# Two-layer hybrid trunk on one core: MLP down product as seven half-size products after the up products, hidden blocks and weight sums through DRAM and GpSimd; GLA level products of two heads together

## The chip, the cores and the metric

One core of one Trainium2 chip runs the whole program. The metric is device time in microseconds: the median of repeated executions. Lower is better. Engines work side by side, each through its own instructions in order: TensorE (matmuls; in the profile PE, its weight loads PEld), VectorE (DVE), ScalarE (ACT), GpSimd (POOL), and SyncE (SP), which issues the DMAs here.

## What is computed

Two layers over 1024 rows of width 1024. Each layer adds a token mixer (layer 0: forgetting attention and Mamba-2; layer 1: stick-breaking attention and gated linear attention, GLA) and then an MLP with 4096 hidden units; a norm ends it. The parts that the change touches:

```python
def squared_relu_mlp(h, w_up, w_down):
    u = jax.nn.relu(h @ w_up)
    return (u * u) @ w_down

def gla_chunked(q, k, v, log_a):
    ...
    attn = jnp.einsum('bcthk,bcshk,bctshk->bctsh', qc, kc, decay)
    o_intra = jnp.einsum('bctsh,bcshv->bcthv', attn, vc)
    ...
    return (o_intra + o_inter).reshape(b, L, H, V)

        h = h + mix.astype(h.dtype)
        u = rms_norm(h, norm_mlp[i])
        h = h + squared_relu_mlp(u, w_mlp_up[i], w_mlp_down[i]).astype(h.dtype)
```

## The kernel before

All of it stays in fp32 precision by splitting: an operand becomes a rounded part (a cast on ScalarE, line 78, `wh`) and a rest (a subtract on VectorE, line 79, `wl`), and each product takes three matmuls: high x high, high x low, low x high. A full matmul is 128 x 128 weights against 128 x 512 columns.

`mlp` (line 381) runs over 16 groups g of 256 hidden units. For a group, the up product is made from seven half-size products, P1 to P7, in the manner of Strassen and Winograd: P1 and P2 in `first(g)`, then P6, P5, P7, P4, P3 in `rest(g)`, each 12 matmuls in `prod` (line 395). The sums around them (s1, s2, s3, s4 of weight blocks; u2, u3, c11, c22 of results) are VectorE's, in `op` (line 407). `put` squares the rectified block (lines 400, 401) and splits it. The hidden blocks c11, u3, u2, c22 are the four quarters of the group's hidden values: 256 units by two halves of 512 rows.

After that `down(g)` multiplies them with the group's two rows of w_down blocks: 16 outputs (two halves of the columns, eight tiles of 128 rows), each 2 x 3 matmuls (lines 494 to 496), and VectorE adds each output into the resident `h` (line 498). `weights(g)` loads four blocks of w_down and splits them. In the order on TensorE, `first(g + 1)` stands ahead of `down(g)`, so the 96 down matmuls of a group run between P2 of the next group and its P6. After the last group `done(tb)` norms finished rows.

The order on each engine is the program's, rearranged by a list scheduler ahead of time; each engine runs its list strictly in order. Buffers come from pools with fixed numbers: `f` (5 blocks of 128 x 512), `q4` (4 pairs), `raw` (5), `wh` and `wl` (6 each). PSUM has eight banks under the names mm (three), av, sc (two), tr (two). A write into a buffer waits until all readers of its last content are done, a DMA that writes it out among them.

The GLA part (lines 876 to 909) works for two pairs of heads in chunks of 512 rows. For each of seven levels VectorE makes a difference M of cumulated gates (line 881), ScalarE takes two exponentials (884, 885), VectorE multiplies with keys and queries (886, 888), and TensorE multiplies M with itself, four 128-column pieces for the head in rows 0 to 63 and then four for the head in rows 64 to 127 (line 895); VectorE copies the result under a mask (line 900). Line 906 does an eighth product from keys and queries. Projection matmuls of the same layer (line 172) stand between these in TensorE's order.

Of the kernel before, what the change touches and what calls it, by code (L numbers as in the profile page):

```python
# [8 lines left out]
F32 = mybir.dt.float32  # L9
F32R = mybir.dt.float32r  # L10
# [23 lines left out]
class Net:  # L34
# [346 lines left out]
    def mlp(self, pool, h, wu, wd, E, scratch, done, late):  # L381
# [7 lines left out]
        T2, T3, T4 = ([E[:, i, j] for i in range(2)] for j in range(3))  # L389

# [8 lines left out]
        def put(c, hT, hf, m):  # L399
            nc.scalar.activation(c, c, AF.Relu)  # L400
            nc.scalar.activation(c, c, AF.Square)
            if hf not in hT:
                hT[hf] = [self.t(pool, [P, 2, HF], "q4", F32R, bufs=4) for _ in range(2)]
            self.split(hT[hf][0][:, m], hT[hf][1][:, m], c)

        def op(out, a, b, f):
            nc.vector.tensor_tensor(out=out, in0=a, in1=b, op=f)  # L407

# [14 lines left out]
        def first(g):  # L423
# [6 lines left out]
            p1 = F()  # L430
            nc.scalar.copy(p1, prod(get(), A11, B11))
            c11 = F()
# [3 lines left out]
        def rest(g, src, a11, a12, p1, c11, more):  # L436
            a21, a22, s1, s2, S2 = more or second(src, a11)
            hT = {}
# [7 lines left out]
            put(c11, hT, 0, 0)  # L446
# [13 lines left out]
            put(c22, hT, 1, 1)  # L460
# [6 lines left out]
            put(u3, hT, 0, 1)  # L467
            op(u2, u2, P3, ALU.add)
            put(u2, hT, 1, 0)
            return hT  # L470

        def weights(g):
            ws = {}
            for nh in range(2):
                for m in range(2):
                    r = self.raw([(0, HF, wd[g * G + m * P:g * G + (m + 1) * P,
                                             nh * HF:(nh + 1) * HF].unsqueeze(1))], 1, HF)
                    ws[nh, m] = self.wsplit(r, HF)
            return ws

        def down(g, hT, ws):
            last = g == NG - 1
            if last:
                S = scratch()
            order = [(nh, tb) for nh in range(2) for tb in range(NTB)]
            if last:
                order = [(nh, tb) for tb in range(NTB) for nh in range(2)]
            for nh, tb in order:
                ps = self.t(self.ps, [P, HF], "mm", bufs=NB["mm"])
                hf, o = tb // 4, (tb % 4) * P  # L490
                for m in range(2):
                    a, b = (x[:, m, o:o + P] for x in hT[hf])
                    wh, wl = ws[nh, m]
                    nc.tensor.matmul(ps, a, wh, start=m == 0, stop=False)  # L494
                    nc.tensor.matmul(ps, a, wl, start=False, stop=False)  # L495
# [575 lines left out]
```

## Time and profile before

| what | value |
|---|---|
| median of three runs | 2552.37 us (2550.16 to 2552.89) |
| profiled execution | 2552.78 us, its span 2550.9 us |
| TensorE matmuls | 2477.8 us busy, 97% of the span |
| VectorE | 1723.1 us, 68% |
| ScalarE | 1117.9 us, 44% |
| GpSimd | 179.3 us, 7% |
| DMA | 142.93 MB, mean 56 GB/s |
| mean granted TensorE clock | 0.993 |

The span is the time from the first to the last instruction of the profiled execution; 1.9 us lie around it. Busy shares are averages over stages with different limits. Matmuls overlap in the records: one takes 0.39 us from start to modelled end, but the next may start 0.23 us after it, so starts are what to count. The granted clock 1.00 is 2.4 GHz, 0.50 is 1.2 GHz.

### The profile page before, as it was taken

To read this page: it belongs to the slowest core of one execution; us is meant where nothing else is said; L and a number is where in the kernel's file an instruction comes from. 1 tells how busy PE (TensorE), PEld (TensorE's weight loads), DVE (VectorE), ACT (ScalarE), POOL (GpSimd) and SP (SyncE) were. 2 spreads that over 40 slices of the span, in tenths; PEclk is the share of its full clock that TensorE was granted. 3 is DMA by queue.
4 is the path that set the end of the run, shared out by engine and by line. 5 is a ranking of instruction groups with operands and counts; after the bars stand their busy time and mean duration, and the time that the engine had idled before them with its cause. 6 is when DMAs were issued, how large, how long until landed. Compare 5 with 4: busy or idle time off the path is not lost.

```text
span 2550.9 us, 33781 instructions
## 1 busy us (share of the span) xinstructions
PE 2477.8 (97%) x12734; PEld 2024.0 (79%) x12734; DVE 1723.1 (68%) x3056; ACT 1117.9 (44%) x2184; POOL 179.3 (7%) x282
## 2 busy tenths in 40 slices
PE   8999989999999999999998889999999999999998
PEld 7777776988888888888976678777988888888887
DVE  5787857577666666666669993676486666666666
ACT  4577646354232333333457665454252333323233
POOL 1111013000000000000113330000000000000000
PEclk9999998999999999999999999999999999999999
DMA  4212222202111111112211011102211111111112
GB/s 138 62 56 58 99 69 56 83 9 71 49 51 51 49 54 50 50 50 63 103 34 28 26 36 38 42 17 67 92 46 54 48 52 50 50 50 50 50 50 87
DMA packets 159922, 142.93 MB, mean 56 GB/s; under 512 B 14704, under 2 KB 130432, under 8 KB 159760
## 3 DMA queue, kind: packets, MB, share of 16 engines
q1 hardware_dynamic: 159760, 140.79, 18.6%
q8 instruction: 100, 1.64, 0.3%
q14 instruction: 62, 0.51, 0.1%
HBM read 128.11 MB, written 12.65 MB: 55 GB/s over the span
## 4 chain that ended last, share of the span: by engine, by line
PE 40%; issue 5%; DVE 3%; POOL 2%; ACT 1%; POOLq 0%; DVEq 0%; ACTq 0%
PE tr L395 5%; PE mm L172 5%; PE sc L395 5%; PE mm L495 4%; PE mm L494 4%; PE mm L496 4%; PE mm L156 3%; PE sc L172 2%; PE av L395 2%; PE sc L895 2%; POOL rr L790 1%; PE av L172 1%; DVE rr L792 1%; POOL pr L790 1%; POOL rs L123 0%
## 5 line engine op out<-in xcount | busy, mean ns | idle before, releaser
L498 DVE TENSOR_TENSOR h<-h,mm 128x512 f32<-128x512 f32 x512 | 350.1, 685 | 141.2 <-PE mm L496 135.2
L495 PE MATMUL mm<-wl,q 128*128 128x512 f32 x1024 | 403.9, 395 | 0.0
L494 PE MATMUL mm<-wh,q 128*128 128x512 f32 x1024 | 403.1, 394 | 0.0
L496 PE MATMUL mm<-wh,q 128*128 128x512 f32 x1024 | 402.0, 393 | 0.0
L78 ACT CAST wh<-raw 128x512 fp32r<-128x512 f32 (+1 forms) x340 | 210.1, 621 | 349.0 <-PE tr L395 124.2
L79 DVE TENSOR_TENSOR wl<-raw,wh 128x512 fp32r<-128x512 f32 (+1 forms) x340 | 232.7, 687 | 100.4 <-ACT wh L78 95.7
L156 PE MATMUL mm<-U,wh 128*128 128x512 f32 x832 | 279.1, 401 | 0.5 <-ACT xin L651 0.5
L78 ACT CAST wh<-f 128x512 fp32r<-128x512 f32 x128 | 76.4, 619 | 350.3 <-DVE h L498 325.6
L494 PEld LDWEIGHTS mm<-wh,q 128*128 128x128 f32 x1024 | 192.2, 188 | 45.7 <-ACT q L78 0.3
L496 PEld LDWEIGHTS mm<-wh,q 128*128 128x128 f32 x1024 | 192.4, 188 | 44.4
L495 PEld LDWEIGHTS mm<-wl,q 128*128 128x128 f32 x1024 | 192.3, 188 | 44.0
L172 PE MATMUL mm<-wh,U 128*128 128x256 f32 (+2 forms) x992 | 226.6, 312 | 0.2 <-ACT U L78 0.2
L156 PEld LDWEIGHTS mm<-U,wh 128*128 128x128 f32 x832 | 156.8, 190 | 32.2 <-issue 1.1
L172 PEld LDWEIGHTS mm<-wh,U 128*128 128x128 f32 x992 | 163.6, 189 | 14.4 <-issue 4.1
L156 PE MATMUL mm<-U,wl 128*128 128x512 f32 x416 | 167.8, 403 | 0.0
L123 POOL TENSOR_TENSOR rs<-ms,mhalf 128x1 f32<-128x1 f32 (+2 forms) x56 | 38.3, 685 | 1806.0 <-DVE ms L121 1806.0
L395 PE MATMUL tr<-U,wh 128*128 128x512 f32 x496 | 155.1, 394 | 0.0
L172 PE MATMUL mm<-wl,U 128*128 128x256 f32 (+2 forms) x496 | 153.8, 310 | 0.6 <-DVE wl L79 0.6
L395 PE MATMUL sc<-U,wh 128*128 128x512 f32 x480 | 150.4, 395 | 0.0
L78 ACT CAST q<-f 128x512 fp32r<-128x512 f32 x128 | 76.1, 616 | 144.3 <-PE mm L495 143.1
L407 DVE TENSOR_TENSOR f<-f,tr 128x512 f32<-128x512 f32 x124 | 82.4, 684 | 72.0 <-PE tr L395 72.0
L256 PE MATMUL tr<-ident,pr 128*128 128x128 f32 x576 | 100.3, 279 | 22.2 <-DVE pr L793 13.8
(312 smaller groups left out, 4912.3 us busy)
## 6 DMA issues: line engine op xcount, KB each, us to landing
raw<-in_w_mlp_up SPq DMA_DIRECT2D x128, 256.0 KB, 2.8
raw<-in_w_mlp_down SPq DMA_DIRECT2D x128, 256.0 KB, 2.7
raw<-in_w_in_ab SPq DMA_DIRECT2D x40, 256.0 KB, 3.0
raw<-in_w_in_cd SPq DMA_DIRECT2D x40, 256.0 KB, 2.9
xload<-in_x SPq DMA_DIRECT2D x8, 512.0 KB, 4.1
gb<-gd SPq DMA_DIRECT2D x8, 512.0 KB, 4.5
catT<-y SPq DMA_DIRECT2D x32, 128.0 KB, 2.2
h<-in_x SPq DMA_DIRECT2D x8, 512.0 KB, 6.2
```

The costliest lines, as they stand in the source:

```text
L78: self.nc.scalar.copy(hi, src)
L79: self.nc.vector.tensor_tensor(out=lo, in0=src, in1=hi.bitcast(F32), op=ALU.subtract)
L156: nc.tensor.matmul(ps, a, b[hf][:, kc], start=kc == 0 and i == 0, stop=kc == NKC - 1 and i == 2)
L172: nc.tensor.matmul(d, a, b, start=kc == 0 and i == 0, stop=kc == NKC - 1 and i == 2)
L256: nc.tensor.transpose(ps[:, k * P:(k + 1) * P], probs[k][:, j * P:(j + 1) * P], self.ident)
L395: nc.tensor.matmul(ps, a[:, kc], b[:, kc], start=kc == 0 and i == 0, stop=kc == 3 and i == 2)
L407: nc.vector.tensor_tensor(out=out, in0=a, in1=b, op=f)
L494: nc.tensor.matmul(ps, a, wh, start=m == 0, stop=False)
L495: nc.tensor.matmul(ps, a, wl, start=False, stop=False)
L496: nc.tensor.matmul(ps, b, wh, start=False, stop=m == 1)
L498: nc.vector.tensor_tensor(out=s, in0=s, in1=ps, op=ALU.add)
L790: nc.gpsimd.affine_select(d, d, [[-1, P]], ALU.is_gt, f, base=0, channel_multiplier=1)
```

## The change

**Up products.** `put` no longer splits. It writes c11, u3 and c22 to DRAM tiles `hid` (A11, A12, A22). After P3 GpSimd makes four sums of hidden blocks, t1 = u2 + c22, t2 = t1 - c11, t4 = u3 - t2, and c11 - u2; they are written to DRAM as S1, S2, S4, S3: seven blocks of 256 KB for each group. `down` and `weights` leave the loop. P1 and c11 now share a `q4` pair.

**Down product.** After all 16 groups a new `down` makes seven products over all 4096 hidden units, in the order S3, S1, S2, A22, A11, S4, A12. Six have 16 steps of 12 matmuls (one step for each group, summed in four PSUM banks); the last has two halves of 16 steps of 6. Each step loads its hidden block back from DRAM and a block of w_down (two for S3 and S1, 512 KB), in the products S3, S1, S2 and A22 GpSimd makes a difference of w_down blocks, and both operands are split (two casts, two subtracts). Up to three steps are split ahead. At the end of a product its banks are added into `h` or subtracted, 56 operations a layer in place of 256. `keep` holds 16 weight sums between products.

**GLA.** `intra` takes the two heads of a pair together, 128-column pieces in turn, into both sc banks. The level difference goes from VectorE to GpSimd, with three buffers gM in place of two. The output products of a chunk are regrouped. The value projection of layer 1 takes its row tiles in the order 4 to 7, 0 to 3.

```diff
@@ mlp
+        hid = {x: [self.t(self.dram, [P, HF], f"hid{x}{g}") for g in range(NG)]
+               for x in ("A11", "A12", "A22", "S1", "S2", "S3", "S4")}
...
-        def put(c, hT, hf, m):
+        def put(c, to, g):
             nc.scalar.activation(c, c, AF.Relu)
             nc.scalar.activation(c, c, AF.Square)
-            if hf not in hT:
-                hT[hf] = [self.t(pool, [P, 2, HF], "q4", F32R, bufs=4) for _ in range(2)]
-            self.split(hT[hf][0][:, m], hT[hf][1][:, m], c)
+            if to is not None:
+                nc.sync.dma_start(hid[to][g], c)
...
-            p1 = F()
+            two = self.t(pool, [P, 2, HF], "q4", bufs=4)
+            p1, c11 = two[:, 0], two[:, 1]
...
-            put(u2, hT, 1, 0)
-            return hT
...
+            put(u2, None, g)
+            two = self.t(pool, [P, 2, HF], "q4", bufs=4)
+            t1, t2, t4 = two[:, 0], two[:, 1], F()
+            pool_op(t1, u2, c22, ALU.add)
+            pool_op(t2, t1, c11, ALU.subtract)
+            pool_op(t4, u3, t2, ALU.subtract)
+            pool_op(u2, c11, u2, ALU.subtract)
+            for to, x in (("S1", t1), ("S2", t2), ("S4", t4), ("S3", u2)):
+                nc.sync.dma_start(hid[to][g], x)
...
-            hT = rest(g, *cur)
-            ws = weights(g)
+            rest(g, *cur)
             if g + 1 < NG:
                 cur = first(g + 1)
-            down(g, hT, ws)
+        self.down(pool, h, wd, hid, scratch, done)
...
+        def t3(k):
+            x = two(wd[k * G:(k + 1) * G, HF:].rearrange("(m p) c -> p m c", p=P))
+            return sub(x[:, 1], x[:, 1], x[:, 0])
...
+        plan = [("S3", t3, [(1, 0, ADD), (1, 1, ADD)]),
+                ("S1", t1, [(0, 1, ADD), (1, 1, ADD)]),
+                ("S2", t2, [(0, 1, ADD), (1, 0, ADD), (1, 1, ADD)]),
+                ("A22", t4, [(1, 0, SUB)]),
+                ("A11", lambda k: block(k, 0, 0), [(1, 0, ADD), (1, 1, ADD), (0, 0, ADD), (0, 1, ADD)]),
+                ("S4", lambda k: block(k, 1, 1), [(0, 1, ADD)]),
+                ("A12", lambda k: block(k, 1, 0), [(0, 0, ADD)])]
...
+        sets = [(mm, mm, mm, self.av), (self.sc, self.sc, self.tr, self.tr)]
+        steps = [(i, 0, 4, k) for i in range(6) for k in range(NG)]
+        steps += [(6, a, 2, k) for a in (0, 2) for k in range(NG)]
...
+            while len(ready) < 3 and s + len(ready) < len(steps):
+                ready.append(operands(*steps[s + len(ready)]))
...
+            for hf, nh, f in plan[i][2]:
+                for j in range(n):
+                    y = h[4 * hf + a + j][:, nh * HF:(nh + 1) * HF]
+                    nc.vector.tensor_tensor(out=y, in0=y, in1=ps[j], op=f)
@@ GLA
+            ps = [net.sc().rearrange("p (c l) -> p c l", l=P) for _ in range(2)]
+            for c in range(4):
+                for hh in range(2):
+                    rows, cs = slice(hh * 64, hh * 64 + 64), slice(c * P, (c + 1) * P)
+                    nc.tensor.matmul(ps[hh][:, c], kx[rows, cs], qx[rows, cs],
+                                     start=True, stop=True)
...
-                M = t(pool, [P, HF], "gM", bufs=2)
+                M = t(pool, [P, HF], "gM", bufs=3)
...
-                nc.vector.tensor_tensor(out=mv, in0=hv,
+                nc.gpsimd.tensor_tensor(out=mv, in0=hv,
...
@@ layer 1
-            for tb in range(NTB):
+            for tb in (4, 5, 6, 7, 0, 1, 2, 3):
```

Where the change moves instructions, in three places.

VectorE at the end of a group's up product, before: the first row is u2 += P3, then three splits of hidden blocks (`q4`) and one of weights; s1 is the row of two raw operands, s2 the next of line 407, s3 the last.

```order
1200 L407 TENSOR_TENSOR f_1919_8669<-f_1919_8669,tr_1964_8928 128x512
1201 L79 TENSOR_TENSOR q4_1961_8920<-f_1959_8915,q4_1960_8919 128x512
1202 L79 TENSOR_TENSOR q4_1950_8873<-f_1955_8895,q4_1949_8872 128x512
1203 L79 TENSOR_TENSOR wl_1982_8984<-raw_1978_8977,wh_1981_8983 128x512
1204 L79 TENSOR_TENSOR q4_1961_8920<-f_1919_8669,q4_1960_8919 128x512
1205 L407 TENSOR_TENSOR f_1985_9002<-f_1983_8987,sc_1986_9003 128x512
1206 L407 TENSOR_TENSOR f_2005_9149<-raw_2003_9145,raw_2004_9147 128x512
1207 L498 TENSOR_TENSOR h0_1002_3662<-h0_1002_3662,mm_1987_9017 128x512
1208 L407 TENSOR_TENSOR f_2006_9150<-f_2005_9149,raw_1977_8975 128x512
1209 L407 TENSOR_TENSOR f_2015_9194<-raw_1977_8975,raw_2003_9145 128x512
```

The same place after (another group): u2 += P3 in the first row, then s1, s2, s3 of the next group, then the split of S2 (from s2).

```order
913 L408 TENSOR_TENSOR q4_1634_6863<-q4_1634_6863,tr_1658_6987 128x512
914 L408 TENSOR_TENSOR f_1672_7062<-raw_1670_7058,raw_1671_7060 128x512
915 L408 TENSOR_TENSOR f_1673_7063<-f_1672_7062,raw_1661_7017 128x512
916 L408 TENSOR_TENSOR f_1680_7104<-raw_1661_7017,raw_1670_7058 128x512
917 L79 TENSOR_TENSOR wl_1675_7067<-f_1673_7063,wh_1674_7066 128x512
918 L408 TENSOR_TENSOR q4_1667_7029<-q4_1667_7029,sc_1669_7044 128x512
919 L79 TENSOR_TENSOR wl_1678_7084<-f_1672_7062,wh_1677_7083 128x512
```

The hidden splits and the adds into h are gone from here; row 916, s3, writes the buffer that held c22 of the group before, so it waits for GpSimd's t1 and for the write of A22, and row 917 stands behind it.

SP at the end of a layer's up products, after: writes of the last group's hidden blocks (`hid...15`), a first load of w_down, then reloads of hidden blocks (`f<-hidS3...`).

```order
307 L405 DMA hidA2215_1464_6274<-f_2051_8969 128x512
308 L405 DMA hidA1215_1448_6258<-f_2047_8949 128x512
309 L504 DMA q4_2061_9016<-in_w_mlp_down 128x2x512
310 L480 DMA hidS115_1480_6290<-q4_2055_8999 128x512
311 L480 DMA hidS215_1496_6306<-q4_2055_8999 128x512
312 L480 DMA hidS415_1528_6338<-f_2056_9000 128x512
313 L480 DMA hidS315_1512_6322<-q4_2030_8855 128x512
314 L540 DMA f_2058_9010<-hidS30_1497_6307 128x512
315 L540 DMA f_2064_9023<-hidS31_1498_6308 128x512
316 L504 DMA q4_2067_9029<-in_w_mlp_down 128x2x512
```

Before, SP had only loads of w_down blocks here (`raw<-in_w_mlp_down`, four for the last group); now the first reload, row 314, stands behind four writes that wait for GpSimd's sums.

VectorE at the end of product A11, after: the split of the second step of the product S4, the adds of A11 into h, and the splits of the third step. The 16 adds are rows 1324 to 1339; the middle ones are left out.

```order
1322 L79 TENSOR_TENSOR wl_2567_11051<-f_2565_11048,wh_2566_11050 128x512
1323 L79 TENSOR_TENSOR wl_2570_11057<-raw_2568_11054,wh_2569_11056 128x512
1324 L562 TENSOR_TENSOR h4_1006_3666<-h4_1006_3666,mm_2477_10696 128x512
1325 L562 TENSOR_TENSOR h5_1007_3667<-h5_1007_3667,mm_2478_10697 128x512
...
1338 L562 TENSOR_TENSOR h2_1004_3664<-h2_1004_3664,mm_2479_10698 128x512
1339 L562 TENSOR_TENSOR h3_1005_3665<-h3_1005_3665,av_2480_10699 128x512
1340 L79 TENSOR_TENSOR wl_2573_11091<-f_2571_11088,wh_2572_11090 128x512
1341 L79 TENSOR_TENSOR wl_2576_11097<-raw_2574_11094,wh_2575_11096 128x512
```

Before, such adds stood one at a time between other work, one for every six down matmuls; now they stand together between the splits of two steps.

TensorE in a GLA level: before, four matmuls of one head and four of the other; after, in 28 of the 32 such places, three, three, one, one (in four they alternate singly). First before, then after.

```order
6558 L172 MATMUL mm_3359_15903<-wl_3284_15553,U_3_76 128x512
6559 L895 MATMUL sc_3314_15636<-gM_3313_15630 128x128 x4
6560 L895 MATMUL sc_3315_15642<-gM_3313_15630 128x128 x4
6561 L172 MATMUL mm_3359_15903<-wh_3283_15552,U_3_76 128x512
6562 L172 MATMUL mm_3359_15903<-wh_3286_15558,U_3_76 128x512
```

```order
6387 L172 MATMUL mm_3772_16612<-wh_3693_16255,U_3_76 128x512
6388 L941 MATMUL sc_3727_16345<-gM_3726_16339 128x128 x3
6389 L941 MATMUL sc_3728_16346<-gM_3726_16339 128x128 x3
6390 L941 MATMUL sc_3727_16345<-gM_3726_16339 128x128
6391 L941 MATMUL sc_3728_16346<-gM_3726_16339 128x128
6392 L172 MATMUL mm_3772_16612<-wh_3696_16261,U_3_76 128x512
```

What moved is that the second head's matmuls now begin before the first head's are all issued.

## Rows read from the trace of the kernel before

**Rows 1.** Page, part 1: span; busy us, share, instructions of each engine.
```profile
span 2550.9 us, 33781 instructions
PE 2477.8 (97%) x12734; PEld 2024.0 (79%) x12734; DVE 1723.1 (68%) x3056; ACT 1117.9 (44%) x2184; POOL 179.3 (7%) x282
```

**Rows 2.** Page, part 5: line, engine, out<-in, count, busy, mean ns, idle before.
```profile
L498 DVE TENSOR_TENSOR h<-h,mm 128x512 f32<-128x512 f32 x512 | 350.1, 685 | 141.2 <-PE mm L496 135.2
...
L496 PE MATMUL mm<-wh,q 128*128 128x512 f32 x1024 | 402.0, 393 | 0.0
L78 ACT CAST wh<-raw 128x512 fp32r<-128x512 f32 (+1 forms) x340 | 210.1, 621 | 349.0 <-PE tr L395 124.2
L79 DVE TENSOR_TENSOR wl<-raw,wh 128x512 fp32r<-128x512 f32 (+1 forms) x340 | 232.7, 687 | 100.4 <-ACT wh L78 95.7
```

**Rows 3.** Chain of waits, one group's first two up products: start, us, what.
```profile
2006.54 5.55 PE tr L395 x24
```

**Rows 4.** Stretches: busy us of PE, PEld, DVE, ACT, POOL; PEclk; DMA share, GB/s.
```profile
2006.50:2048.20 41.70, 41.70 (x182) 33.87 (x181) 26.93 (x43) 13.92 (x24) 0.00 (x0) 1.00 0.17 51
...
1627.00:1673.00 46.00, 45.36 (x326) 36.24 (x324) 38.74 (x73) 16.99 (x34) 0.00 (x0) 1.00 0.04 12
...
369.50:375.60 6.10, 0.06 (x1) 0.00 (x0) 0.82 (x3) 2.36 (x10) 0.78 (x1) 0.83 0.77 176
375.60:387.20 11.60, 11.60 (x36) 8.64 (x37) 5.11 (x9) 8.46 (x23) 1.98 (x3) 0.50 0.60 93
433.80:435.80 2.00, 0.04 (x2) 0.03 (x1) 1.18 (x3) 1.98 (x6) 0.72 (x2) 0.79 0.38 56
435.80:445.30 9.50, 9.45 (x33) 8.07 (x34) 6.79 (x12) 5.53 (x15) 1.46 (x2) 0.51 0.18 31
304.00:306.00 2.00, 1.69 (x13) 1.54 (x13) 2.00 (x4) 0.98 (x2) 0.00 (x0) 1.00 1.02 416
```

**Rows 5.** Timeline in the MLP, TensorE and VectorE: start, us, what, [idle before].
```profile
2037.05 0.69 DVE L79 TENSOR_TENSOR wl<-f,wh 128x512 fp32r<-128x512 f32 x1 [0.65 <-ACT wh L78]
2037.65 0.68 DVE L498 TENSOR_TENSOR h<-h,mm 128x512 f32<-128x512 f32 x1
...
2045.00 0.40 PE L496 MATMUL mm<-wh,q 128*128 128x512 f32 x1
...
2045.44 0.69 DVE L498 TENSOR_TENSOR h<-h,mm 128x512 f32<-128x512 f32 x1 [0.70 <-PE mm L496]
```

**Rows 6.** Groups of one MLP group's stretch: ScalarE's relu and square.
```profile
L400 ACT ACTIVATE f<-f 128x512 f32<-128x512 f32 x4 | 2.4, 627 | 2.8 <-DVE f L407 2.8
L401 ACT ACTIVATE f<-f 128x512 f32<-128x512 f32 x4 | 2.4, 624 | 0.1
```

**Rows 7.** Timeline in the Mamba-2 part: GpSimd and VectorE side by side.
```profile
406.52 1.05 POOL L705 TENSOR_TENSOR xdt<-xt,dtT 128x512 f32<-128x512 f32 x1 [1.65 <-PE av L737]
407.64 1.37 POOL L711 TENSOR_TENSOR xt<-xt,dsk 128x512 f32<-128x512 f32 x1
...
406.87 1.24 DVE L748 TENSOR_TENSOR xt<-xt,zs 128x512 f32<-128x512 f32 x1
```

**Rows 8.** Timeline in stick-breaking attention: VectorE follows a GpSimd result.
```profile
1311.57 0.29 POOL L790 TENSOR_SCALAR_AFFINE_SELECT rr<-rr 128x128 f32<-128x128 f32 x1 [65.75 <-ACT rr L785]
...
1311.90 1.55 DVE L792 TENSOR_TENSOR_SCAN rr<-rr 128x640 f32<-128x640 f32 x1 [0.53 <-POOL rr L790]
```

**Rows 9.** Timeline of SP in the MLP: one issue of a load.
```profile
2057.89 0.34 SPq L90 DMA_DIRECT2D raw<-in_w_mlp_down  x1
```

**Rows 10.** Page, part 6: DMA, count, KB each, us from issue to landing.
```profile
raw<-in_w_mlp_down SPq DMA_DIRECT2D x128, 256.0 KB, 2.7
```

**Rows 11.** Timeline of TensorE, matmuls on 64 rows in GLA and in Mamba-2.
```profile
1649.96 1.71 PE L895 MATMUL sc<-gM 64*128 64x128 f32 x16
1651.60 0.49 PE L923 MATMUL tr<-qs,v 128*128 128x128 f32 x2
...
388.36 0.70 PE L716 MATMUL sc<-state,CT 64*128 64x256 f32 x4
388.99 0.50 PE L172 MATMUL mm<-wh,U 128*128 128x512 f32 x1
```

More of the change, by code (lines that the diff above doesn't have):

```diff
@@ L437, in rest @@
             a21, a22, s1, s2, S2 = more or second(src, a11)
-            hT = {}
             late_next()
@@ L445, in rest @@
             P5 = prod(self.tr() if g else mm(), S1, T1)
-            put(c11, hT, 0, 0)
+            put(c11, "A11", g)
             s3 = F()
@@ L459, in rest @@
             op(c22, u3, P5, ALU.add)
-            put(c22, hT, 1, 1)
+            put(c22, "A22", g)
             s4 = s2
@@ L466, in rest @@
             op(u3, u3, P4, ALU.add)
-            put(u3, hT, 0, 1)
+            put(u3, "A12", g)
             op(u2, u2, P3, ALU.add)
-            put(u2, hT, 1, 0)
-            return hT
[L472 to L495, printed above, removed]
-                    nc.tensor.matmul(ps, b, wh, start=False, stop=m == 1)
-                s = h[tb][:, nh * HF:(nh + 1) * HF]
-                nc.vector.tensor_tensor(out=s, in0=s, in1=ps, op=ALU.add)
-                if last and nh == 1:
-                    done(tb, S)
+            put(u2, None, g)
@@ L871, in gla, with intra @@
         el = [t(pool, [P, 4], f"el{i}", bufs=1) for i in range(2)]
+        def intra(i, lev, kx, qx):
+            ps = [net.sc().rearrange("p (c l) -> p c l", l=P) for _ in range(2)]
[4 more added lines that the diff above has]
+                                     start=True, stop=True)
+            mk = msk[:, lev].unsqueeze(1).broadcast_to([P, 4, P])
+            for hh in range(2):
+                if lev == 0:
+                    nc.vector.tensor_tensor(out=aT[i][:, hh], in0=ps[hh], in1=mk, op=ALU.mult)
+                else:
+                    nc.vector.copy_predicated(aT[i][:, hh], mk.bitcast(I32), ps[hh])
         for i in range(2):
@@ L889, in gla @@
                                         op=ALU.mult)
[L890 to L909 removed]
+                intra(i, lev, M, M)
+            intra(i, 7, gk[i][:, hs], gq[i][:, hs])
             nc.scalar.activation(qd[i], H4, AF.Exp, scale=-IG)
@@ L920, in gla @@
             for h in range(4):
-                i, lo = h // 2, (h % 2) * 64
-                vv = v[cc][:, h * P:(h + 1) * P]
-                nc.tensor.matmul(o[h % 2][:, i], aT[i][:, h % 2, c], vv, start=True, stop=cc == 0)
-                if cc > 0:
+                nc.tensor.matmul(o[h % 2][:, h // 2], aT[h // 2][:, h % 2, c],
+                                 v[cc][:, h * P:(h + 1) * P], start=h < 2, stop=cc == 0,
+                                 skip_group_check=True)
+            if cc > 0:
+                for h in range(4):
+                    i, lo = h // 2, (h % 2) * 64
                     nc.tensor.matmul(o[h % 2][:, i], qd[i][lo:lo + 64, c], state[lo:lo + 64, i],
-                                     start=False, stop=True)
+                                     start=False, stop=True, skip_group_check=True)
             os = t(pool, [P, HF], "os", bufs=2)
```

74 lines of the change are left out of this document (53 added, 21 removed).

## The prediction

> **What bounds the kernel now.** I read the page's first part, then its groups, then the chain of waits and the table by stretches. TensorE is busy 97% of the span [rows 1]. In the MLP the groups of the down product show no idle time in front of any matmul, while the adds into h sit idle for 141 us, waiting for TensorE [rows 2]. The chain of one hidden group confirms it: 24 matmuls in 5.55 us, so 0.231 us from one 128x512 matmul to the next, whatever their ends say [rows 3]; in the 41.70 us of a whole group TensorE is busy for 41.70, VectorE for 26.9, ScalarE for 13.9, GpSimd not at all, and the DMA engines are used to 0.17 [rows 4]. So a matmul taken out of the MLP is worth 0.231 us, as long as nothing else starts to end last. The reader should see two more things. A group's 96 down matmuls are 22 us of cover between the last product of one group and the first use of the next group's sums. And the two GLA stretches are bound by TensorE too (45.4 us of 46.0), because projection matmuls fill every hole [rows 4].
>
> **The change, part by part.** Times are added to the profiled execution, 2552.8 us; the median of the three runs is 2552.4, so nothing has to be corrected between them.
>
> *Fewer matmuls.* A layer's down product is 16 x 96 = 1536 matmuls now. After: six products of 16 x 12 and one of 2 x 16 x 6, together 1344. 192 fewer a layer, 384 in all, x 0.231 = **-89 us**. This is a count, and its bounds are narrow; what follows is what eats it.
>
> *The up products without cover.* Set T at the end of a group's P3. A result is with VectorE 0.2 us after the next matmul starts: the matmul of 2045.00 releases the add of 2045.44 [rows 5]. Then u2 += P3 (to 0.9), relu and square at 0.62 each [rows 6] (to 2.2), the GpSimd sum t1, 1.05 [rows 7] (to 3.25). The next VectorE instruction in order, s3 of the next group, wants t1's operand back, and the split of S2 stands behind it; P6 wants that split. TensorE meanwhile has P1 and P2 of the next group, 5.55 us, and needs the split of S2 at its third matmul, T + 6.0. VectorE and GpSimd take turns: an operation of VectorE with two operands in SBUF that began at 406.87 took 1.24 us and ended 0.6 after the GpSimd operation beside it, and the next GpSimd operation took 1.37 in place of 1.05 [rows 7]. The Trainium skill, "SBUF — State Buffer", section "Who interferes with whom", says the same: a VectorE instruction with two SBUF inputs contends with a GpSimd instruction that reads SBUF, and the later one blocks; the trace agrees, by that 1.24. So it matters who is first when t1 ends. VectorE follows a GpSimd result by 0.04 us (1311.86 to 1311.90) [rows 8], GpSimd follows its own by 0.07 (407.57 to 407.64) [rows 7]: VectorE is ahead, s3 runs to 3.95, GpSimd's t2 to 5.0, the split of S2 to 5.65, and TensorE does not wait. If GpSimd wins, t2 goes first (4.35), s3 (5.0), the third sum (6.0), the split (6.65): 0.65 us a group, 20 us for the 30 group changes; with t1 late by one VectorE operation (0.6) it is 1.3, or 39. I take **+2**, bounds 0 and 39.
>
> *From up to down, once a layer.* After the last P3 nothing is left for TensorE. The four GpSimd sums end at 2.2 + 4 x 1.05 = 6.4; SP holds their writes in order ahead of the first reload of a hidden block, 0.34 an issue [rows 9], so that reload is issued at 7.2. It lands 2.7 later (same size, w_down blocks [rows 10]), then cast 0.62 and subtract 0.69 [rows 2]: 11.2 us, against a third matmul 0.5 after the first. About 11 us of idle TensorE, **+22** for two layers; the writes in front of the read can add 1 to 2 each.
>
> *The clock.* After 6.1 us nearly without matmuls the granted clock was 0.50 for 11.6 us, after 2.0 us for 9.5 us [rows 4]: 1.2 GHz in place of 2.4, half the work, so 5.8 and 4.8 us lost. I expect it behind the two long gaps and the two of the next paragraph: **+18**, bounds 3 and 25.
>
> *Steps and product ends of the down product.* A step of 12 matmuls is 2.78 us. In it VectorE has two subtracts, starting 0.60 apart [rows 5], ScalarE two casts (1.24), GpSimd one operation in the products S3, S1, S2 and A22 (1.05), SP two issues (0.7). VectorE and GpSimd in turn make 2.25: it fits. Loads are 256 + 512 KB a step in S3 and S1, 786,000 bytes in 2.78 us, 283 GB/s; the trace reaches 416 at a share of 1.02 [rows 4]: it fits, with a third to spare. At a product's end its adds stand on VectorE ahead of the split that the next product's third step needs (the order at A11 is in the section on the change). TensorE has two steps, 5.55 us, and wants that split 0.25 into the third, 5.8. The adds begin while the last step still runs, so four are done 0.8 after it. Eight adds: 3.2, plus two splits 1.3: 4.5, no wait. Twelve (S2): 6.9, 1.1 of wait. Sixteen (A11): 9.3, 3.5 of wait. 4.6 a layer, **+10** with rounding for a GpSimd turn; bounds 5 and 20.
>
> *Last product in halves, ends of layers.* Steps of 6 matmuls, 1.39 us, against about 1.0 each of VectorE and ScalarE, with the norms of finished rows between them. **+4**, bounds 0 and 10.
>
> *GLA.* 28 level subtracts leave VectorE (28 x 0.60 = 17 us of an engine that is busy 38.7 of 46) and go to GpSimd. On TensorE one level is 16 instructions in 1.64 us (next one of another line at 1651.60) [rows 11]. Alternating 64-row halves do better: the four instructions of 388.36, with twice the columns, gave way after 0.63 us, 0.08 for 128 columns against 0.10 [rows 11]. But the new order puts three matmuls of one head and then three of the other in most of the levels, so only two pairs meet. 0.1 to 0.4 us for 32 levels, 3 to 13: **-8**. Below: -22, if the halves overlap in full. Above: +15, because both banks must now be free before a level starts, and a GpSimd subtract of 1.05 can stand ahead of two VectorE products. The Trainium skill, "TensorE: Matmul & The Clock Gate", section "The mechanism", lets matmuls on different rows of the array run side by side with starts a few nanoseconds apart; the trace shows a gain of a fifth only. By the page the GLA term would be -26 and the time 2494. The order of layer 1's value projection only moves evictions: nothing.
>
> **Sum:** -89 + 2 + 22 + 18 + 10 + 4 - 8 = -41: **2512 us**.
>
> **The rivals.**
> 1. *Nearly the whole gain arrives.* Short gaps leave the clock alone (4 in place of 18), product ends cost 5, the chain of the up products nothing, GLA gives 20: -89 + 20 + 4 + 5 + 1 - 20 = -79, **2474**. For it: VectorE and ScalarE have slack nearly everywhere. Against it: both gaps of [rows 4] fell to half clock, and mine are longer. Chance 0.18.
> 2. *GpSimd's sums stretch every group (the slow side).* Place: the split of S2 behind s3 and behind t2 and its followers. If t1 is late by one operation and three GpSimd sums get ahead of the split, it ends at 8.35, a wait of 2.3 us a group, 69 us: **2579**. It decides against the change from 43 / 30 = 1.4 us a group. For it: turn-taking is in the trace, and the race is decided by 0.03 us. Against: to lose 1.4 several turns must go wrong in each group, and the trace shows VectorE served at once when it has waited. Chance 0.12.
> 3. *DMA.* If loads of 2 KB rows beside others come at 230 GB/s, a step of S3 and S1 takes 3.4 us, 64 x 0.63 = 40, and the half steps of A12 (393,000 bytes in 1.39) 64 x 0.3 = 20: **2572**. The 416 GB/s speak against. Chance 0.08.
> 4. *GLA gives nothing back* (+15 in place of -8): **2535**. Chance 0.12.
>
> That the change does not do what it says is excluded: the order has 1344 down matmuls a layer.
>
> **How the numbers follow.** The forecast (chance 0.50) has its own range 2495 to 2540. The range for 8 in 10 reaches to rival 1 below and to most of 2 and 3 above: 2474 to 2575. About 0.2%, 5 us, is what a measurement of this kernel can tell from no change. Faster than 2547: 0.46 of the forecast's 0.50, all of rival 1, most of 4: 0.74. Within 5 us: upper end of the forecast, low end of 2: 0.08. Slower: rivals 2 and 3: 0.18.
>
> **What will show it.** In the profile of the changed kernel: 384 fewer matmuls, the same 0.231 between them; in the up products no TensorE idle time with the subtract of S2 (L79, wl from f) as releaser, or 0.65 or more of it a group (rival 2); one gap of about 11 us a layer before the first down matmul and a granted clock of 0.5 behind it; 1 us and 3.5 us of wait at the ends of S2 and A11; a DMA share of about 0.7 in S3 and S1, near 1.0 if rival 3 holds; in the GLA stretches a shorter time for the same matmuls, with VectorE less busy. Wrong it would be made above all by the up products, where 1 us a group is 30 us.

## The result and the profile after

The changed kernel takes 2522.9 us (median of four, 2519.3 to 2529.1) against 2552.6: a ratio of 0.989, 95% interval 0.987 to 0.991, so 29 us less. The forecast was 2512, 41 less, and its range held the time.

The page, part 1, after (span, then busy time, share and instructions of each engine), beside [rows 1]:

```profile
span 2521.0 us, 35516 instructions
...
PE 2400.1 (95%) x12350; PEld 1952.7 (77%) x12350; DVE 1754.6 (70%) x2884; ACT 1246.5 (49%) x2438; POOL 608.0 (24%) x566
```

384 matmuls are gone (12734 to 12350), as counted. But the span fell by 30 us and not by 89, and TensorE is busy 95% of it in place of 97%: some 60 us went into time in which it waits or runs at a lower clock. Where? The MLP of layer 0 took 678 us from the start of its first up matmul to that of its last down matmul and now takes 666; layer 1's 671 and 661; the stretch between the two, GLA in it, 636 and 628. Unrounded, 12.0 + 10.6 + 7.6 make the 30; the start and the end of the program cancel out.

What TensorE waits for in layer 0's down product, six of the seven products (who waited for whom: sum, times, longest):

```profile
PE mm L553 <- ACT wh L78: 12.4, 1, 12.4
PE sc L553 <- DVE wl L79: 6.2, 5, 3.3
PE mm L553 <- DVE wl L79: 3.3, 2, 3.0
```

One wait of 12.4 us before the first down matmul, and 9.5 us in seven waits for VectorE's subtracts. Layer 1 shows the same (12.2, 6.2, 4.0). The stretches (busy us of PE, PEld, DVE, ACT, POOL, then granted clock, DMA share, GB/s) of the way from up to down, of the product S1, of A11, and of S4, against [rows 4]:

```profile
873.00:886.40 13.40, 1.04 (x5) 0.54 (x3) 1.52 (x3) 2.62 (x5) 6.18 (x5) 0.68 0.65 215
...
933.40:981.00 47.60, 45.58 (x194) 35.75 (x192) 45.23 (x39) 18.31 (x33) 37.45 (x25) 1.00 0.77 259
1077.00:1121.00 44.00, 44.00 (x191) 35.59 (x190) 22.41 (x37) 17.95 (x32) 0.00 (x0) 1.00 0.60 190
1121.50:1172.00 50.50, 47.21 (x192) 37.70 (x191) 34.55 (x57) 21.79 (x40) 3.11 (x4) 0.93 0.59 193
```

A11 is what the prediction meant by a step that fits: TensorE busy all the time, VectorE half of it. S1 is not: VectorE is busy 45.2 us of 47.6, GpSimd 37.5. DMA does not bound any of them; in S3 the share was 0.94 at 328 GB/s while loads ran ahead, and after its first down matmul TensorE had no wait for a load.

### The profile page after: what moved, and what is told of

Same layout as the page of the kernel before. It is cut to its first block, busy times and chain, and to the rows that moved or that the text cites. A ratio compares the mean times of both kernels' runs of the same rounds, so it can differ in the third digit from the quotient of the medians.

```text
span 2521.0 us, 35516 instructions
## 1 busy us (share of the span) xinstructions
PE 2400.1 (95%) x12350; PEld 1952.7 (77%) x12350; DVE 1754.6 (70%) x2884; ACT 1246.5 (49%) x2438; POOL 608.0 (24%) x566
## 3 DMA queue, kind: packets, MB, share of 16 engines
q8 instruction: 97, 1.59, 0.3%
## 5 line engine op out<-in xcount | busy, mean ns | idle before, releaser
L79 DVE TENSOR_TENSOR wl<-f,wh 128x512 fp32r<-128x512 f32 (+1 forms) x384 | 362.3, 949 | 197.3 <-ACT wh L78 194.0
L78 ACT CAST wh<-f 128x512 fp32r<-128x512 f32 (+1 forms) x384 | 218.4, 585 | 440.3 <-PE av L553 163.8
L553 PE MATMUL mm<-wh,wh 128*128 128x512 f32 x384 | 153.9, 401 | 24.5 <-ACT wh L78 24.5
L553 PE MATMUL mm<-wl,wh 128*128 128x512 f32 x384 | 155.8, 406 | 7.5 <-DVE wl L79 7.4
L553 PE MATMUL mm<-wh,wl 128*128 128x512 f32 x384 | 153.3, 399 | 0.0
L411 POOL TENSOR_TENSOR q<-q,f 128x512 f32<-128x512 f32 x32 | 41.3, 1289 | 435.3 <-ACT q L403 435.3
L397 PEld LDWEIGHTS tr<-U,wh 128*128 128x128 f32 x496 | 93.2, 188 | 21.7
L172 PE MATMUL sc<-wh,U 128*128 128x256 f32 (+1 forms) x560 | 109.0, 285 | 0.2
L78 ACT CAST ph<-tr 128x512 fp32r<-128x512 f32 x192 | 87.3, 481 | 42.6 <-PE tr L256 40.7
L553 PEld LDWEIGHTS mm<-wh,wh 128*128 128x128 f32 x384 | 73.6, 192 | 43.2 <-ACT wh L78 25.6
```

What stands on the lines that cost most here:

```text
L78: self.nc.scalar.copy(hi, src)
L79: self.nc.vector.tensor_tensor(out=lo, in0=src, in1=hi.bitcast(F32), op=ALU.subtract)
L172: nc.tensor.matmul(d, a, b, start=kc == 0 and i == 0, stop=kc == NKC - 1 and i == 2)
L397: nc.tensor.matmul(ps, a[:, kc], b[:, kc], start=kc == 0 and i == 0, stop=kc == 3 and i == 2)
L411: nc.gpsimd.tensor_tensor(out=out, in0=a, in1=b, op=f)
L553: nc.tensor.matmul(ps[j], l[:, cs], r, start=k == 0 and x == 0, stop=k == NG - 1 and x == 2)
```

## Experiments

Ratios are those to the kernel before, taken on the same chip in the same runs; the changed kernel's is 0.9887. A difference of ratios of 0.001 is 2.6 us. Where a run is set against the changed kernel, both intervals count, and the difference is known to about 6 us.

### The two parts by themselves

The kernel before with the GLA part alone:

```diff
-                for hh in range(2):
-                    ...
-                        nc.tensor.matmul(ps[:, c], m, m, start=True, stop=True)
+                intra(i, lev, M, M)
...
-                nc.vector.tensor_tensor(out=mv, in0=hv,
+                nc.gpsimd.tensor_tensor(out=mv, in0=hv,
```

> The kernel before with only the GLA part of the change (heads together, level difference on GpSimd, regrouped output products, order of layer 1's value projection); the MLP as before. Theory: the GLA term of the prediction, -8, is real and independent of the MLP: 8 us faster than before, 2545, the stretch from the end of layer 0's down product to the start of layer 1's up product 7 to 8 us shorter. Rival: the gain seen in that stretch came from the new MLP (its earlier end, other buffers): then within 2 us of before.

Measured: 0.9970 (0.9959 to 0.9981), 7.7 us faster. The stretch between the MLPs took 627.0 us against 635.9, so the rival, that the gain came from the new MLP, is out.

The changed kernel with the GLA part as before:

```diff
-                intra(i, lev, M, M)
+                for hh in range(2):
+                    ...
+                        nc.tensor.matmul(ps[:, c], m, m, start=True, stop=True)
```

> The changed kernel with the GLA part as before. Theory: the two MLPs alone give 11 to 12 us a layer, so 22 us faster than before, 2530. Rival: the parts help each other, then the two experiments do not add up to the 30 us of the whole change.

Measured: 0.9909 (0.9897 to 0.9922), 23 us faster. 7.7 + 23 is 31, the whole change 29: within the intervals the parts add up, and neither needs the other.

### The up products: who is first when t1 ends

The step on which rival 2 rested can be read in the changed kernel. T, the end of a P3, is at 600.57. VectorE, GpSimd and TensorE from there (start, us, what, [idle before and its releaser]):

```profile
600.77 0.69 DVE L408 TENSOR_TENSOR q<-q,tr 128x512 f32<-128x512 f32 x1 [1.86 <-PE tr L397]
...
604.19 0.69 DVE L408 TENSOR_TENSOR f<-raw,raw 128x512 f32<-128x512 f32 x1 [1.40 <-POOL q L411]
604.80 1.79 DVE L79 TENSOR_TENSOR wl<-f,wh 128x512 fp32r<-128x512 f32 x1
...
602.87 1.29 POOL L411 TENSOR_TENSOR q<-q,f 128x512 f32<-128x512 f32 x1 [12.90 <-ACT q L403]
604.23 1.80 POOL L411 TENSOR_TENSOR q<-q,q 128x512 f32<-128x512 f32 x1
...
606.62 0.40 PE L397 MATMUL tr<-U,wh 128*128 128x512 f32 x1
606.86 0.39 PE L397 MATMUL tr<-E,wl 128*128 128x512 f32 x1
```

u2 += P3 begins 0.20 after T, t1 at 2.30, and s3 (604.19) follows t1's end (604.16) by 0.03, ahead of t2 (604.23) by 0.04: the order that the forecast chose. The subtract of S2 then stands behind t2 and takes 1.79 us in place of 0.69, t2 1.80 in place of 1.29. It ends at T + 6.0, where I had 5.65, since a sum takes 1.29 us on GpSimd and not the 1.05 of [rows 7]. All 30 group changes look like this one: s3 begins 0.03 us and t2 0.08 after the end of t1, and the split ends 2.43 or 2.44 after it.

Why 1.29? The two rows of [rows 7] are multiplications, but that is not what makes them cheap. One operand of each is broadcast (`dtT` and `dsk` have one value for 64 columns), and the level difference of GLA, a subtraction with a broadcast operand, costs as little on GpSimd, while the sums here read two full operands (groups: count, busy, mean ns). That the broadcast makes the difference is argued from these, not tested:

```profile
L958 POOL TENSOR_TENSOR gM<-v 128x512 f32<-128x512 f32 x28 | 30.0, 1074 | 136.0 <-DVE v L911 51.9 <-DVE wl L79 39.4 <-PE sc L941 34.4
...
L411 POOL TENSOR_TENSOR q<-q,f 128x512 f32<-128x512 f32 x2 | 2.6, 1288 | 37.8 <-ACT q L403 37.8
```

The matmul that needs the split (606.86, the one on `wl`) starts without a wait, but with some luck. I had counted it as the third behind P1 and P2; the scheduler put one of P5 ahead of it (606.62), so it is the fourth. In the third place it would have come 0.04 us after the split's end, and 0.05 is the least that a matmul follows such a split in these runs. As it is, it follows by 0.09 to 0.27 in the 30 group changes. To see how near that is to the edge, t1 was made twice:

```diff
             pool_op(t1, u2, c22, ALU.add)
+            pool_op(t1, u2, c22, ALU.add)
             pool_op(t2, t1, c11, ALU.subtract)
```

> The changed kernel with the sum t1 of every hidden group made twice on GpSimd (same operands, same result). Theory (turn-taking of VectorE and GpSimd): the chain from P3 to the split of S2 has 0.35 us to spare, s3 waits for the second t1, 1.1 later, so TensorE waits 0.7 us in each of 30 group changes: 21 us slower than the changed kernel, 2544, with the subtract of S2 as releaser. Rival 1 (no turn-taking, more to spare): the split ends 0.6 earlier than I worked out, and nothing or under 5 us is lost, 2525. Rival 2 (turns lost to GpSimd when it has more to do): 1.3 us or more a group, 2560 or more.

Measured: 0.9992 (0.9983 to 1.0001), 27 us slower than the changed kernel: the gain is gone. One group change there, VectorE, GpSimd, TensorE:

```profile
626.18 0.69 DVE L408 TENSOR_TENSOR f<-raw,raw 128x512 f32<-128x512 f32 x1 [2.78 <-POOL q L411]
...
623.48 2.66 POOL L411 TENSOR_TENSOR q<-q,f 128x512 f32<-128x512 f32 x2 [12.38 <-ACT q L403]
626.22 1.81 POOL L411 TENSOR_TENSOR q<-q,q 128x512 f32<-128x512 f32 x1
...
627.69 0.40 PE L397 MATMUL sc<-E,wh 128*128 128x512 f32 x1
628.63 0.50 PE L397 MATMUL tr<-E,wl 128*128 128x512 f32 x1 [0.55 <-DVE wl L79]
```

s3 is released by the second t1, 1.4 later than before, the subtract of S2 ends 1.4 later, and the matmul on `wl` starts 0.94 after its neighbour in place of 0.23: 0.7 us lost, in eight of the 30 groups 1.1 to 1.5 in all. (The scheduler moved things here too: one add of VectorE stands ahead of the split, which still ends 2.43 after t1, and the matmul on `wl` is the sixth.) The up products of the two layers, which had 5.7 and 6.6 us over their matmuls, 5.1 and 6.4 of it in the first group, now have 19.9 and 20.1: 28 us. So the chain was the one I had worked out, with hardly anything to spare, and 1.3 us more of GpSimd uses up the whole gain. Rival 1 of this experiment, that there was slack to hide it, is out; the 0.9 us a group are also short of rival 2, turns lost to GpSimd, which wanted 1.3 or more.

### The waits that were not foreseen

The prediction had waits behind S2 (1.1) and A11 (3.5). They came, 1.06 and 3.45. It had none behind S3 and S1, where 1.45 and 3.15 us were lost in each layer. VectorE, then GpSimd, at the end of S1 and the start of S2:

```profile
979.36 1.77 DVE L79 TENSOR_TENSOR wl<-E,wh 128x512 fp32r<-128x512 f32 x1
981.06 1.78 DVE L79 TENSOR_TENSOR wl<-f,wh 128x512 fp32r<-128x512 f32 x1
982.76 1.78 DVE L79 TENSOR_TENSOR wl<-E,wh 128x512 fp32r<-128x512 f32 x1
984.46 1.27 DVE L562 TENSOR_TENSOR h<-h,sc 128x512 f32<-128x512 f32 x2
...
989.25 0.72 DVE L79 TENSOR_TENSOR wl<-f,wh 128x512 fp32r<-128x512 f32 x1
...
970.31 16.65 POOL L508 TENSOR_TENSOR E<-raw,E 128x512 f32<-128x512 f32 x10
```

Ten GpSimd operations in 16.65 us, one after the other; they are weight sums for S2, made while S1 runs. With them one subtract of VectorE at a time, eight in all, 1.70 us from one to the next. Two a step make 3.4 us, and a step of TensorE is 2.78. I had counted one GpSimd operation a step; but GpSimd runs ahead as far as loads and buffers let it, and while it does, every subtract of VectorE meets one. So VectorE enters the end of the product with no lead, and the adds, with one operand in PSUM and 0.60 each also beside GpSimd, come on top. With GpSimd's weight sums on VectorE:

```diff
         def sub(out, a, b):
-            nc.gpsimd.tensor_tensor(out=out, in0=a, in1=b, op=ALU.subtract)
+            nc.vector.tensor_tensor(out=out, in0=a, in1=b, op=ALU.subtract)
```

> The changed kernel with the weight sums of the down product on VectorE in place of GpSimd (64 a layer); the hidden sums of the up products stay on GpSimd. Theory: the waits of 1.4 us at the start of S1 and 3.1 us at the start of S2, which the prediction did not have, come from GpSimd running its sums in bursts as the loads arrive, so that each VectorE subtract takes 1.78 us in place of 0.68; without GpSimd there they go, the one behind S2 grows by 0.6, the one behind A11 stays: 8 us less of these waits in two layers, 3 us less of half clock, about 2 us less of small holes: 12 us faster than the changed kernel, 2511. Rival: VectorE is short of time as such, and a third operation in each step makes all waits at product ends longer: 4 us slower, 2527.

Measured: 0.9823 (0.9810 to 0.9836), 16 us faster than the changed kernel. The stretch of S1 there:

```profile
935.97:980.50 44.53, 44.53 (x193) 36.02 (x192) 40.97 (x67) 18.32 (x32) 0.00 (x0) 1.00 0.84 295
```

TensorE is busy all of 44.5 us, where S1 took 47.6. VectorE does a third operation in every step and is busy 4 us less, so the rival, that VectorE is short of time as such, is out. The wait behind S3 is gone, that behind S1 is 0.3 and 0.8, those behind S2 and A11 stayed at 1.1 and 3.5. So the turns with GpSimd have no part in the last two. Dealing out the adds takes these:

```diff
+            for f in todo[:2]:
+                f()
+            del todo[:2]
...
-                    nc.vector.tensor_tensor(out=y, in0=y, in1=ps[j], op=f)
+                    todo.append(lambda y=y, p=ps[j], f=f:
+                                nc.vector.tensor_tensor(out=y, in0=y, in1=p, op=f))
```

> The changed kernel with the adds into h of a finished product dealt out, two to each of the next product's steps, in place of all at once (the last product's halves still at once). Theory: the waits in the third step of a product (1.4, 3.1, 1.1 and 3.5 us a layer, 18 us in two) are the block of adds between two splits; dealt out, those behind S2 and A11 go (9 us), those behind S3 and S1 shrink, as far as GpSimd's bursts allow, and 5 us of half clock with them: 15 us faster than the changed kernel, 2508. Rival: the waits are VectorE's lack of time as such: dealt out they come back as small holes of the same sum, 2522.

Measured: 0.9822 (0.9808 to 0.9837), 17 us faster than the changed kernel. Its A22 and A11 in one stretch, and its S4, for which the changed kernel took 50.5:

```profile
1032.10:1121.00 88.90, 88.90 (x384) 71.99 (x383) 50.44 (x81) 36.49 (x64) 0.00 (x0) 1.00 0.47 150
1121.30:1165.80 44.50, 44.50 (x193) 36.05 (x192) 34.84 (x58) 21.95 (x40) 2.17 (x4) 1.00 0.68 221
```

No wait is left behind S2 and A11, and the clock stays at 1.00, where it had fallen to 0.5 for 6.8 us behind A11. The wait behind S3 is gone too, and of the 3.15 us behind S1 1.8 remained; in S1 there are three waits of 0.5 to 0.7, which the run with both edits (below) no longer has. So behind S2 and A11 the block of adds alone ended last; behind S3 and S1 it was block and turns together, and either edit takes away all of the first and much of the second.

### From up to down

The chain after the last P3 of layer 0 in the changed kernel, VectorE, GpSimd (first sum), SP (reloads), ScalarE, TensorE:

```profile
873.78 0.69 DVE L408 TENSOR_TENSOR q<-q,tr 128x512 f32<-128x512 f32 x1 [2.11 <-PE tr L397]
...
875.87 1.26 POOL L411 TENSOR_TENSOR q<-q,f 128x512 f32<-128x512 f32 x1 [12.91 <-ACT q L403]
...
881.78 0.93 SPq L540 DMA_DIRECT2D f<-hidS  x2
...
884.91 0.62 ACT L78 CAST wh<-f 128x512 fp32r<-128x512 f32 x1 [9.12 <-DMA f<-hidS]
...
886.10 0.79 PE L553 MATMUL mm<-wh,wh 128*128 128x512 f32 x1 [12.36 <-ACT wh L78]
```

The links are those of the forecast; the reload is issued 8.2 us after T and not 7.2, again for the 1.26 of a GpSimd sum. The first matmul on the new operands has a granted clock of 0.5. Three steps loaded and split ahead should have closed the gap:

```diff
             S4 = self.wsplit(s4, HF)
             late_next()
+            if ahead:
+                ahead()
```

> The changed kernel with the loads and splits of the first three steps of the down product ahead of the last group's P3 and its writes. Theory: the gap of 12.3 us a layer is the chain VectorE, ScalarE, four GpSimd sums, four writes in SP's order, reload, split; with three steps ready the gap goes but for 2 to 3 us in front of the fourth step, whose reload still stands behind the writes, and most of the half clock behind it: 20 us and 4 us less, 2498. Rival: TensorE waits there for something else (banks, the writes of S3 to land): then the gap stays at 10 us or more and the time at 2520.

Measured: 0.9864 (0.9852 to 0.9877), 6 us faster than the changed kernel, no more than the two intervals allow; 24 were expected. SP, then ScalarE and VectorE, in the same place:

```profile
873.30 0.33 SPq L90 DMA_DIRECT2D raw<-in_w_mlp_down  x1
873.68 0.90 SPq L493 DMA_DIRECT2D f<-hidS  x2
...
889.86 0.94 SPq L562 DMA_DIRECT2D f<-hidS  x2
```

```profile
877.47 0.62 ACT L78 CAST wh<-f 128x512 fp32r<-128x512 f32 x1 [5.20 <-DMA f<-hidS]
...
881.74 0.68 DVE L408 TENSOR_TENSOR q<-q,tr 128x512 f32<-128x512 f32 x1
```

The edit did not do what it was meant to. SP issued the early reloads only at 873.68, behind loads of w_down that it held in order, 0.2 us after the last P3. ScalarE and VectorE stood in order at their splits, so u2 += P3 ran at 881.74, 8 us late, and with it the sums, the writes and the reload of the fourth step (889.86). The gap fell from 12.8 to 5.4 us, and a wait of 4.7 us came before the fourth step; gap and S3 together took 59.0 us against 60.1 in layer 0, and 61.4 against 60.4 in layer 1. That the chain is the one named is confirmed in a way (delayed by 8 us, it delays the fourth step), but not that the gap can be closed; what the two MLPs gained lies elsewhere, 1.2 us a layer in S1 (the wait behind S3 cost 0.7 in place of 1.45) and 2.0 in S2, where the wait of 3.0 stayed but no half clock followed it, and I can't say why. A reload ahead of SP's blocked loads was not tried.

### GLA

The two halves of that part alone, in the kernel before. Heads together, the difference left on VectorE:

```diff
-                for hh in range(2):
-                    ...
-                        nc.tensor.matmul(ps[:, c], m, m, start=True, stop=True)
+                intra(i, lev, M, M)
```

> The kernel before with only the two heads of a GLA level taken together and the output products regrouped; the level difference stays on VectorE with two buffers. Theory: the GLA stretches are bound by TensorE, so the gain of the change's GLA part is the overlap of 64-row matmuls: 5 to 8 us faster than before, 2546. Rival: VectorE bound them: then the difference on GpSimd was the gain, and this gives 0 to 2 us, or loses up to 10 since a level now needs both banks free.

Measured: 1.0005 (0.9996 to 1.0014), no change, where 5 to 8 us less were expected. The difference on GpSimd with three buffers, heads apart:

```diff
-                nc.vector.tensor_tensor(out=mv, in0=hv,
+                nc.gpsimd.tensor_tensor(out=mv, in0=hv,
```

> The kernel before with only the level difference of GLA on GpSimd and three buffers; heads one after the other. Theory: VectorE was not what bounded the stretches, so 0 to 2 us faster than before, 2551. Rival: VectorE bounded them: 6 to 8 us faster, 2545.

Measured: 1.0140 (1.0119 to 1.0160), 36 us slower. Neither theory nor rival had that. The stretches of this run (columns as above):

```profile
1628.00:1636.00 8.00, 7.39 (x56) 5.86 (x54) 5.61 (x10) 2.55 (x6) 2.13 (x2) 1.00 0.22 68
1636.00:1687.00 51.00, 51.00 (x233) 43.69 (x235) 29.66 (x52) 10.40 (x31) 12.65 (x12) 0.50 0.00 1
```

For 51 us TensorE is busy without a hole and runs at 1.2 GHz; a second such stretch has 24 us. Half of 75 is the loss. Before the clock fell, TensorE had done three levels with single projection matmuls between them and two waits for VectorE (0.43 and 0.18 us); in the stretch there is mostly one projection matmul for a level of sixteen 64-row instructions, so the order that the scheduler made of this edit uses the projection matmuls elsewhere. That this is why the clock fell is not shown. The run with the heads alone has 17 us at half clock at the end of the part (1745 on), which costs 8.5 us at most; whether the heads gain that much is not shown either, for when the clock fell the 29th level had begun 113.9 us after the first, against 113.0 in the kernel before. With both halves together no clock is lost inside the GLA stretch. So what each half is worth by itself these runs do not say: each has such a stretch.

What the heads bring by themselves can be read in the changed kernel, where the first level alternates singly and the next has three, three, one, one (TensorE):

```profile
1615.99 1.16 PE L941 MATMUL sc<-gM 64*128 64x128 f32 x16
1617.09 0.50 PE L172 MATMUL mm<-wh,U 128*128 128x512 f32 x1
...
1618.03 1.66 PE L941 MATMUL sc<-gM 64*128 64x128 f32 x16
1619.62 0.50 PE L172 MATMUL mm<-wh,U 128*128 128x512 f32 x1
```

1.10 us from the first instruction to the next line's when they alternate, 1.59 when they are grouped, 1.64 before [rows 11]. Singly they run fully side by side: one of each head 0.006 us apart and the next pair 0.11 later, as long as one instruction alone takes in the level of [rows 11]; all sixteen start within 0.89 us, before within 1.44. So single alternation takes a third off the 1.64 of a level, where I had read a fifth from four instructions with twice the columns. That reading was wrong, not the row: the four of 388.36 also start in pairs, 0.007 apart. But 28 of 32 levels don't get it. The Trainium skill, "TensorE: Matmul & The Clock Gate", section "The mechanism", has matmuls on different rows run side by side. The trace agrees in full where they alternate singly; in the level of [rows 11], four and four, only three of eight pairs do. An attempt to give it to them by holding the order:

```diff
-                    nc.tensor.matmul(ps[hh][:, c], kx[rows, cs], qx[rows, cs],
-                                     start=True, stop=True)
+                    with net.tc.issue_after(last) if last else nullcontext():
+                        last = nc.tensor.matmul(ps[hh][:, c], kx[rows, cs], qx[rows, cs],
+                                                start=True, stop=True).ins
```

> The changed kernel with the two heads' pieces of a GLA level held strictly in turn on TensorE (head 0, head 1, head 0, ...), where the changed kernel has three, three, one, one in 28 of 32 levels. Theory: 64-row matmuls on different halves run fully side by side only when they alternate (0.89 us for a level's 16 instructions, against 1.2 to 1.4 as grouped and 1.44 before): 0.35 us in 28 levels, 9 us faster than the changed kernel, 2514. Rival 1: the projection matmuls between the levels run out and the granted clock falls to 0.5 in the stretch, as in the experiment with the difference alone on GpSimd: 0 to 15 us slower. Rival 2: VectorE's chain sets the period of a level (2.45 us), and the shorter block only makes TensorE wait: no change.

Measured: 0.9899 (0.9883 to 0.9916), 3 us slower than the changed kernel, within what the two intervals allow, where 9 us faster were expected. The stretch between the MLPs took 632.3 us against 628.2. The clock stayed at 1.00 through the levels, so rival 1 is not the reason, and levels follow each other at 3.0 to 3.1 us in place of 2.4 to 2.5, so rival 2, a fixed period, is not either. The order held, but the scheduler put the first matmul of a level ahead by itself, with projection matmuls behind it:

```profile
1618.33 0.46 PE L943 MATMUL sc<-gM 64*128 64x128 f32 x2
1618.71 0.50 PE L172 MATMUL mm<-wh,U 128*128 128x512 f32 x1
...
1619.37 1.16 PE L943 MATMUL sc<-gM 64*128 64x128 f32 x14
1620.45 0.73 PE L172 MATMUL mm<-wh,U 128*128 128x512 f32 x2
```

0.38 and 1.08 us: 1.46 for a level. Fourteen take 0.88 us from first to last start, as sixteen in one piece did, and cutting a level in two costs about 0.4 us in the changes between matmuls on 64 and on 128 rows (1.46 against 1.10). A level of 1.1 us in all places was not had, so its worth stays open.

### Together

Weight sums on VectorE and adds dealt out:

> The changed kernel with the weight sums of the down product on VectorE and the adds into h dealt out over the next product's steps. Theory: the first removes the waits behind S3 and S1 and small holes of S1, the second those behind S2 and A11, each with its half clock; they add up but for about 2 us that both remove: 28 to 30 us faster than the changed kernel, 2493 to 2496. Rival: with three operations and two adds in a step VectorE has 3.0 us for 2.78 of TensorE in the first half of a product, and 2 us a product come back: 2510.

Measured: 0.9756 (0.9741 to 0.9772), 2490.1 us, 33 us faster than the changed kernel, the sum of both within the intervals, and without half clock behind any product end. (In the traces the two MLPs are 29 us shorter, where the two edits alone give 13 and 19: what both remove counts once.) The products S1, S2, A22, A11 and S4 of layer 0 take 44.6 us each, their 192 matmuls and nothing else. With the early splits of three steps as well:

> As the run before, and the first three steps of the down product loaded and split ahead of the last group's P3. Theory: the gains add: 6 us more, 2488. Rival: the reload ahead of the writes competes with the last up loads: no gain over the run before.

Measured: 0.9754 (0.9739 to 0.9770), 2489.7 us: no gain over the run before, as its rival had it; the early splits again move the wait instead of removing it (gap 5.3 and a wait of 4.6 in place of 13.0). With the GLA order held on top:

> As the run before, and the GLA heads strictly in turn. Theory: 9 us more, 2479, the best of all. Rivals as for the GLA heads alone.

Measured: 0.9787 (0.9771 to 0.9803), 2498.8 us, 9 us slower than the run before, where 9 faster were expected. 6.5 us of it lie in the stretch between the MLPs (634.1 against 627.6), so the held order is a loss here, as the 4 us of the run with it alone had hinted. The best two, 2490, beat both kernels: 62 to 63 us below the kernel before, where the change by itself gave 29.

## Why the prediction was right, and by how much each term was off

- *Fewer matmuls* (-89): 384 fewer, 0.231 apart. Right.
- *Up products without cover* (+2): nothing lost in 30 group changes. Right, with the order of s3 and t2 as argued, but in part by luck: the price of a GpSimd sum (1.05, from rows with a broadcast operand, really 1.29) was wrong and used up the 0.35 us that I believed to be spare, and a matmul of P5 ahead of the one that waits gave 0.23 back. Rival 2 was nearer than 0.12 says: 1.3 us more in the chain cost 27 us.
- *From up to down* (+22): 12.4 and 12.2, 24.6. Right, 1.2 us a layer short, most of it for the same GpSimd price.
- *Clock* (+18): half clock under running matmuls for 5.4, 3.4 and 6.0 us in layer 0 and 4.0, 3.4 and 3.4 in layer 1, 25.6 us, so 13 lost. The gaps drew it as [rows 4] had shown; much of the two long stretches lay in the gap itself, where it costs nothing.
- *Steps and product ends* (+10): mis-sized, 18 at four product ends a layer, 9 of it foreseen, and some 7 of small waits in the products with GpSimd's sums and after them. The two ends that I had worked out came to a tenth of a microsecond; the failing step is "VectorE and GpSimd in turn make 2.25: it fits", which takes one GpSimd operation to a step. With ten in a row every VectorE subtract waited for a turn, 3.4 us a step. The experiment with the sums on VectorE removed it.
- *DMA* (rival 3): no wait for a load in the down product's steps. Out.
- *GLA* (-8): 7.7 alone. The size was right. The reason that I gave, TensorE with VectorE second, is only partly shown. Levels follow each other at 2.4 us in the first half and 2.9 in the second, where they took 2.9 and 3.4. On TensorE the 32 blocks, from each of their instructions to the next start, take 49.7 us in place of 54.7: 5 us, most of it 0.05 to 0.2 a level and 0.55 where a level alternates singly. Where the other 2 to 3 us come from is open, and neither half alone gained anything.
- *Last product in halves, ends of layers* (+4): about 4 is left for the rest of the account, but not where I put it. The last product and the ends of the layers cost 1 us more than before and the program's end 1.3; some 3 us are lost in the first groups of the up products, half of that in layer 1 under 3.4 us of half clock (1854.0 to 1857.4), which the kernel before does not have there. The start of the program was 1 us shorter.

The sum of 41 was 11 too good: 15 more at the ends and in the steps of the products and 2.6 more in the gaps, against 5 less of clock and 2 less in the up products.

## What to carry to other kernels

Matmuls taken out of a kernel that TensorE bounds also take out cover: find each chain that they hid, work it out instruction by instruction, and write down what it has to spare. An engine that runs ahead is to be counted at the rate at which it can run, not at the rate at which it is needed, as soon as it shares something with the engine that the bound waits for. And look at the waits of a version that already gained: here moving 128 small operations back and dealing out the adds gave 33 us, more than the change itself. A price read from a row holds for operands like those of the row.

## What was not expected of the hardware

TensorE's clock fell to 0.50 for 51 us in a stretch without any hole, busy 51.0 of 51.0 us with 64-row matmuls of 128 columns and a few of 512; I had looked for it behind gaps only. With two full operands a 128x512 sum or difference takes GpSimd 1.26 to 1.30 us, with one of them broadcast about 1.05, a product [rows 7] as well as GLA's difference (1.07 in the mean, turns with VectorE included). And the turn-taking of VectorE and GpSimd is strict over long stretches: eight subtracts of VectorE beside GpSimd's sums, 1.70 us from one to the next.
